# A hybrid encoder layer on one core: an operand split ahead, a transpose later, a gating step more, values loaded under the head before

## The chip, the cores and the metric

The kernel runs on one core of one Trainium2 chip. The metric is the time of one execution on the device in microseconds (us). The core has five engines with an instruction stream each, worked off in the order written: TensorE (PE in the profile; its weight loads are PEld), VectorE (DVE), ScalarE (ACT), GpSimd (POOL) and SyncE (SP). DMAs are issued from the streams of ACT, POOL and SP. An engine that meets an instruction whose semaphore has not come stands, and everything behind it in its stream stands too.

## The reference, cut to what matters

One layer over 1024 tokens (16 rows of 64 columns) with 2048 channels, float32:

```python
h = rms_norm(x, pre_g)
q, k, v, z_a, u, vs, z_b, g_a, g_b = split(h @ w_in)      # 1024 x 7 and 2048 x 2 columns
y_a = neighbourhood_attention(q, k, v, rpb) * silu(z_a)   # 8 heads of 128, window 8 x 16
y_b = u * (W_s layer_norm(vs) + b) * silu(z_b)            # 8 groups of 128, chunks of 128 tokens
merged = sigmoid(g_a) * (y_a @ w_pa) + sigmoid(g_b) * (y_b @ w_pb)
out = x + rms_norm(merged @ w_out, post_g)
```

## The kernel before, in words

Every float32 operand of the large products is split into a rounded part `wh` and a rest `wl` (ACT casts in line 120, DVE subtracts in line 121), and each product is made of three matmuls: high by high, high by low, low by high. A *step* is one such product of 512 contraction rows by 512 tokens: 12 matmuls in line 153. The columns of `w_in` are worked in pairs of 128; a pair takes 7 steps (a Strassen form with results in the PSUM banks A, B and C), a few pairs take 8 plain ones. There are 732 steps. After them the output projection runs in line 1001. The weights of a pair are loaded by SP a pair ahead (line 141), split two steps before their use, and results leave the banks by ACT (line 202, 292) and DVE (line 197); POOL's DMAs (line 293) store them to DRAM, the second half of the contraction being added there to the first.

The main loop (line 1024) writes one step after the other. In each it writes the evacuation of the step before, then for the first steps a piece of `first_builds` (the activations' operand tiles `a`: ACT scales `y` into the high part in line 411, DVE makes the low part in line 412), then one `hook()`, which advances the first of the waiting *tasks* up to its next `yield`, then the matmuls of the step, and then the split of weights two steps on. So a `yield` in a task is a distance of one step between what stands before and after it, on all engines at once. The tasks in order:

- `norms` (line 453): squares and sums of x, then `r_cols` = 1/rms by a DVE reduction (line 469) and a GpSimd power (line 116), then three small TensorE transposes (lines 473 and 483), DVE copies (475, 484), and a round trip over DRAM that spreads the result as `r_rows`.
- `values`, `layer_norms`: transposes of v and vs.
- `gating(g)` for 8 groups (line 557): loads `z` (a group ahead) and `u` from `d_zu`; first step: a matmul with `ones` (567) and z times r_rows (571); second step: Silu of z, the loads of the next group's z, and u times r_rows (578); third and fourth step: one half each of the chunk matmuls (583), the products (585, 587, 590) and the store. u is loaded by POOL (line 492) in the first step.
- `attention` (line 617): 8 heads, 11 steps each (`i` from 0 to 10): scores of block i (683), normalised (696), transposed (704) and, three steps after the scores, weighted with the values (716). A head's values come by four POOL loads (659) into one tile `vk`, issued ahead of `i` = 0. At `i` = 2 POOL loads the gate `za` (665), which DVE scales at `i` = 4 (751); at `i` = 3 it loads the next head's q and k, and from `i` = 7 on these are scaled and split (`prelude`).

```python
            fetch_values(h)
            following = None
            for i in range(11):
                if i >= 3:
                    weighted(h, i - 3)
```

`prepare_upto(k)` (line 1014) splits weights up to step k-1; before, the first call stands behind the first piece of `first_builds`.

Of the kernel before, what the change touches and what calls it, by code (L numbers as in the profile page):

```python
# [17 lines left out]
P = 128  # L18
# [75 lines left out]
def hybrid_kernel(ctx: ExitStack, tc: tile.TileContext, x, x_t, pre_g, post_g, w_vs, w_v, w_units, bias, ln_g, ln_b,  # L94
# [358 lines left out]
    def norms():  # L453
        pool = Pool(tc, "npool")
        ss = pool.tile([P, T // P, 2], F32, "ss")
        halves = {}
        for j in range(17):
            if j < 16:
                t, e = divmod(j, 2)
                halves[j] = pool.tile([P, T], F32, "xn", bufs=2)  # L460
                nc.sync.dma_start(out=halves[j], in_=x[t * P:(t + 1) * P, e * T:(e + 1) * T])
            yield
            if j > 0:
                t, e = divmod(j - 1, 2)
                src = halves.pop(j - 1)
                junk = pool.tile([P, T], BF16, "junk")
                nc.scalar.activation(junk, src, AF.Square, accum_out=ss[:, t, e:e + 1])
            yield
        nc.vector.tensor_reduce(out=r_cols, in_=ss, op=ALU.add, axis=AX.X)
        rsqrt_into(r_cols, r_cols, 1.0 / D, RMS_EPS)  # L470
        yield
        pt = psum("t")
        nc.tensor.transpose(out=pt[:T // P, :P], in_=r_cols, identity=ident)
        rows = pool.tile([T // P, P], F32, "rows")
        nc.vector.tensor_copy(rows, pt[:T // P, :P])
        nc.sync.dma_start(out=r_dram, in_=rows)
        nc.sync.dma_start(out=r_rows, in_=r_dram.rearrange("t p -> (t p)").partition_broadcast(P))

        for dst, src in ((lng, ln_g), (lnb, ln_b)):
            by_group = pool.tile([G, P], F32, "by_group", bufs=2)  # L480
            nc.scalar.dma_start(out=by_group, in_=src.rearrange("(g p) -> g p", p=P))
            pt = psum("t")
            nc.tensor.transpose(out=pt[:, :G], in_=by_group, identity=ident[:G, :G])
            nc.vector.tensor_copy(dst, pt[:, :G])
        yield
        pool.close()
# [62 lines left out]
    def fetch_group(g):  # L549
        z = [block(bpool, ("zu", g), 0, hf, "z", 4) for hf in range(2)]  # L550
        wst = bpool.tile([P, P], F32, "wst", bufs=2)
        nc.sync.dma_start(out=wst, in_=ws_t[:, g, :])
        bs = bpool.tile([P, 1, P], F32, "bs", bufs=2)
        nc.sync.dma_start(out=bs, in_=b_s[g:g + 1, :].partition_broadcast(P))
        fetched[g] = z, wst, bs

    def gating(g):

        if g not in fetched:
            fetch_group(g)  # L560
            yield
            yield
        z, wst, bs = fetched.pop(g)
        u = [block(bpool, ("zu", g), 1, hf, "u", 2) for hf in range(2)]

        pb = psum("t")
        nc.tensor.matmul(pb[:, :P], lhsT=ones, rhs=wst, start=True, stop=True)
        nc.vector.scalar_tensor_tensor(out=bs[:, 0], in0=pb[:, :P], scalar=lnb[:, g:g + 1], in1=bs[:, 0],
                                       op0=ALU.mult, op1=ALU.add)
        for hf in range(2):  # L570
            nc.vector.tensor_tensor(out=z[hf], in0=z[hf], in1=r_rows[:, hf * HALF:(hf + 1) * HALF], op=ALU.mult)
        yield
        for hf in range(2):
            nc.scalar.activation(z[hf], z[hf], AF.Silu)
        if ("zu", g + 1) in complete:
            fetch_group(g + 1)
        for hf in range(2):
            nc.vector.tensor_tensor(out=u[hf], in0=u[hf], in1=r_rows[:, hf * HALF:(hf + 1) * HALF], op=ALU.mult)
        yield
        for hf in range(2):  # L580
            po = psum("t")
            for i in range(4):
                nc.tensor.matmul(po[:, i * P:(i + 1) * P], lhsT=vn[hf * 4 + i][:, g * P:(g + 1) * P],
                                 rhs=wst, start=True, stop=True)
            nc.vector.tensor_tensor(out=u[hf], in0=u[hf], in1=z[hf], op=ALU.mult)
            yb = bpool.tile([P, HALF], F32, "yb", bufs=2)
            nc.vector.scalar_tensor_tensor(
                out=yb.rearrange("p (c s) -> p c s", s=P), in0=po.rearrange("p (c s) -> p c s", s=P),
                scalar=lng[:, g:g + 1], in1=bs.broadcast_to([P, 4, P]), op0=ALU.mult, op1=ALU.add)
            nc.vector.tensor_tensor(out=yb, in0=yb, in1=u[hf], op=ALU.mult)  # L590
            nc.gpsimd.dma_start(out=y_dram[8 + g][:, hf * HALF:(hf + 1) * HALF], in_=yb)
            yield
# [24 lines left out]
    def attention():  # L617

        pool = Pool(tc, "p2")
        scale = 128.0 ** -0.5  # L620
        raw, kept, bts = {}, {}, {}
        probs, sums, pv = {}, {}, {}

        def fetch(h):
# [27 lines left out]

            return [lambda: scaled(h, 0), lambda: queries(h), lambda: scaled(h, 1), lambda: keys(h)]

        def fetch_values(h):
            vk = pool.tile([P, 4, 4, P], F32, "vk")
            for b in range(4):
                w = KW[b]
                nc.gpsimd.dma_start(out=vk[:4 * w, b], in_=v_dram[h, :, COL0[b]:COL0[b] + w])
            kept[h].append(vk)  # L660

        def fetch_gate(h):
            zs = pool.tile([P, T], F32, "za")
# [44 lines left out]
        def weighted(h, i):  # L708
            hf, b = QTILES[i]
            n = 4 * KW[b]  # L710
            vk, zs = kept[h][2:]
            pk = probs.pop(("t", i))
            if b == 0:
                pv[hf] = psum("v")
            for rc in range(3):
                nc.tensor.matmul(pv[hf][:, b * P:(b + 1) * P], lhsT=vk[:n, b, ROW0[hf] // 4 + rc, :],  # L716
                                 rhs=pk[:n, rc, :], start=(rc == 0), stop=(rc == 2))
            if b == 3:
                zv = zs.rearrange("p (r b c) -> p b r c", b=4, c=16)[:, :, 8 * hf:8 * hf + 8]
                nc.vector.tensor_tensor(out=zv, in0=pv[hf].rearrange("p (b r c) -> p b r c", b=4, c=16),  # L720
                                        in1=zv, op=ALU.mult)

        for h in range(H):
            if h not in kept:
                while ("head", h) not in complete:
                    yield
                fetch(h)
                for i in range(3):
                    fetch_bias(h, i)
                    yield  # L730
                for f in prelude(h):
                    f()
                    yield
            fetch_values(h)
            following = None
            for i in range(11):
                if i >= 3:
                    weighted(h, i - 3)
                if 2 <= i < 10:
                    transposed(i - 2)  # L740
                if 1 <= i < 9:
                    normalised(i - 1)
                if i < 8:
                    if i < 5:
                        fetch_bias(h, i + 3)
                    scores(h, i)
                if i == 2:
                    fetch_gate(h)
                    zs = kept[h][3]
                if i == 4:  # L750
                    nc.vector.tensor_tensor(out=zs, in0=zs, in1=r_rows, op=ALU.mult)
                if i == 5:
                    nc.scalar.activation(zs, zs, AF.Silu)
                if i == 3 and ("head", h + 1) in complete:
                    fetch(h + 1)
                    following = prelude(h + 1)
                if following and i >= 7:
                    following[i - 7]()
                    if i >= 8:
                        fetch_bias(h + 1, i - 8)  # L760
                yield
            nc.gpsimd.dma_start(out=y_dram[h], in_=zs)
            del kept[h]
# [260 lines left out]
    for k, (n, name) in enumerate(seq):  # L1024
        for f, args in events.pop(k, ()):
            f(*args)
        if k:
            pn, pname = seq[k - 1]
            pairs[pn].evacuate(pname)
            release(k)  # L1030
        if not begun and next(starting, StopIteration) is StopIteration:
            begun = True
            ypool.close()
            begin(norms)
        if k % 4:
            build()
        need(pairs[n].left, PRODUCTS[name][1] if name in PRODUCTS else PlainPair.STEPS[name][1])
        hook()
        prepare_upto(k + 1)
        pairs[n].multiply(name)  # L1040
        prepare_upto(k + 1 + DEPTH)
        if k == len(seq) - 6:
            loaded.extend(load_chunk(n) for n in range(LOADS))
        if k == len(seq) - 1:
            advance(0)
# [163 lines left out]
```

## Time and profile before

| | |
|---|---|
| median of 3 runs | 2528.94 us (2527.4 to 2533.26) |
| the profiled execution | 2526.07 us |
| its span, first to last instruction | 2524.2 us |
| TensorE busy in it | 2485.5 us, 98% |
| VectorE / ScalarE / GpSimd busy | 56% / 42% / 17% |
| mean granted clock of TensorE | 0.996 |

The table is read so: TensorE is busy for nearly all of the span, so time is to be had only from the stretches in which it waits or has a lower clock. Its busy time does not tell the clock: a matmul at the lower level is busy for longer. The profiled execution took 1.9 us more than its span.

### The profile page before, as it was taken

Reading aid. Unit: us, or ns where it says so; the run is one execution under the profiler, and the core shown is the slowest. Engines: PE = TensorE matmul, PEld = TensorE weight load, DVE = VectorE, ACT = ScalarE, POOL = GpSimd, SP = SyncE. Lnnn points to the kernel's source line nnn. Section 1 sums busy time; section 2 is a strip of 40 time slices with the busy share of each in tenths; the row PEclk is TensorE's granted clock in tenths of the full one; section 3 lists DMA queues with packets and bytes.
Section 4 is the critical chain, followed back from the end, with each engine's and each line's share of the span. In section 5 each row is a group of like instructions: output and inputs, shape, how many; then the busy total and the mean of one; then the engine's idle time right before and its main releaser. Section 6 shows DMA issues by size and latency. Waiting matters only on the chain.

```text
span 2524.2 us, 32543 instructions
## 1 busy us (share of the span) xinstructions
PE 2485.5 (98%) x11363; PEld 2063.2 (82%) x11363; DVE 1421.7 (56%) x2284; ACT 1051.1 (42%) x1871; POOL 439.0 (17%) x669
## 2 busy tenths in 40 slices
PE   8999999999999999999999999999999999999998
PEld 6878888888888888887788878888888888888887
DVE  7444444444444754567765655566586787632434
ACT  5533333333334534443366656554443444432332
POOL 0111111111111112123322232233311121200000
PEclk9999999999999999999999999999999999999999
DMA  6643333333335469777778686799865687733635
GB/s 194 205 128 113 115 106 109 115 110 108 114 109 175 110 114 226 161 150 193 174 169 195 152 196 148 180 284 231 226 186 171 225 201 151 230 107 97 210 116 196
DMA packets 237380, 410.14 MB, mean 162 GB/s; under 512 B 31496, under 2 KB 90912, under 8 KB 236576
## 3 DMA queue, kind: packets, MB, share of 16 engines
q1 hardware_dynamic: 163296, 226.56, 30.3%
q0 software_dynamic: 72112, 176.77, 29.0%
q10 hardware_dynamic: 1808, 4.74, 0.5%
q8 instruction: 89, 1.46, 0.2%
q14 instruction: 75, 0.61, 0.1%
HBM read 264.78 MB, written 143.13 MB: 162 GB/s over the span
## 4 chain that ended last, share of the span: by engine, by line
PE 86%; issue 4%; DMA 4%; DVE 3%; ACT 2%; POOL 1%; POOLq 0%; SPq 0%; DVEq 0%; ACTq 0%
PE A L153 39%; PE C L153 20%; PE B L153 10%; PE t L1001 3%; PE A L1001 3%; PE v L1001 2%; PE s L1001 2%; PE C L1001 2%; PE B L1001 2%; DMA vk<-v_dram 1%; PE v L716 1%; DMA u<-d_zu 1%; DVE wl L121 1%; PE s L683 1%; PE t L516 1%
## 5 line engine op out<-in xcount | busy, mean ns | idle before, releaser
L153 PE MATMUL A<-a,wh 128*128 128x512 f32 x3328 | 1034.9, 392 | 10.4 <-ACT wh L120 9.2
L121 DVE TENSOR_TENSOR wl<-x,wh 128x512 fp32r<-128x512 f32 x736 | 505.8, 688 | 660.2 <-ACT wh L120 659.8
L153 PEld LDWEIGHTS A<-a,wh 128*128 128x128 f32 x3328 | 622.7, 189 | 136.1 <-ACT wh L120 9.2
L120 ACT CAST wh<-x 128x512 fp32r<-128x512 f32 x736 | 455.9, 620 | 488.2 <-PE C L153 229.0
L153 PE MATMUL A<-a,wl 128*128 128x512 f32 x1664 | 651.3, 391 | 1.7 <-DVE wl L121 1.7
L153 PE MATMUL C<-a,wh 128*128 128x512 f32 x1664 | 516.4, 392 | 3.5 <-DVE u L197 3.4
L202 ACT COPY u<-A 128x512 f32<-128x512 f32 x300 | 175.8, 586 | 537.3 <-PE A L153 534.9
L153 PEld LDWEIGHTS A<-a,wl 128*128 128x128 f32 x1664 | 313.6, 188 | 71.3 <-DVE wl L121 5.2
L153 PEld LDWEIGHTS C<-a,wh 128*128 128x128 f32 x1664 | 311.1, 188 | 67.0 <-issue 2.8
L153 PE MATMUL C<-a,wl 128*128 128x512 f32 x832 | 325.4, 391 | 2.8 <-DVE wl L121 2.7
L197 DVE TENSOR_TENSOR u<-C,u 128x512 f32<-128x512 f32 x200 | 137.9, 690 | 240.0 <-ACT u L202 149.1
L153 PE MATMUL B<-a,wh 128*128 128x512 f32 x864 | 267.2, 390 | 0.0
L153 PEld LDWEIGHTS B<-a,wh 128*128 128x128 f32 x864 | 161.2, 188 | 32.5
L153 PEld LDWEIGHTS C<-a,wl 128*128 128x128 f32 x832 | 156.6, 188 | 37.2 <-DVE wl L121 4.1
L153 PE MATMUL B<-a,wl 128*128 128x512 f32 x432 | 168.7, 390 | 0.2 <-DVE wl L121 0.2
L174 DVE TENSOR_TENSOR x<-x,x 128x512 f32<-128x512 f32 x200 | 137.7, 688 | 3.5
L120 ACT CAST wh<-s 128x512 fp32r<-128x512 f32 x100 | 62.1, 621 | 107.7 <-PE B L153 105.9
L292 ACT COPY c<-A 128x512 f32<-128x512 f32 x88 | 51.6, 586 | 127.0 <-PE A L153 127.0
L153 PEld LDWEIGHTS B<-a,wl 128*128 128x128 f32 x432 | 81.1, 188 | 18.3 <-DVE wl L121 1.2
L197 DVE TENSOR_TENSOR u<-B,u 128x512 f32<-128x512 f32 x100 | 68.8, 688 | 22.1 <-PE B L153 22.1
L1001 PE MATMUL A<-wh,a 128*128 128x512 f32 x208 | 80.9, 389 | 0.0
L1001 PE MATMUL t<-wh,a 128*128 128x512 f32 x208 | 80.9, 389 | 0.0
(241 smaller groups left out, 2546.0 us busy)
## 6 DMA issues: line engine op xcount, KB each, us to landing
x<-w_units SPq DMA_DIRECT2D x288, 256.0 KB, 2.9
x<-w_out SPq DMA_DIRECT2D x120, 256.0 KB, 2.7
d_zu<-u POOLq DMA_DIRECT2D x48, 256.0 KB, 4.0
d_qk<-u POOLq DMA_DIRECT2D x48, 256.0 KB, 4.0
d_gb<-u POOLq DMA_DIRECT2D x48, 256.0 KB, 3.6
d_ga<-u POOLq DMA_DIRECT2D x48, 256.0 KB, 4.1
m<-u POOLq DMA_DIRECT2D x48, 256.0 KB, 4.3
y<-x_t SPq DMA_DIRECT2D x32, 256.0 KB, 5.3
```

Source lines behind the costliest of these rows:

```text
L120: nc.scalar.copy(out=hi, in_=src)
L121: nc.vector.tensor_tensor(out=lo, in0=src, in1=hi.bitcast(F32), op=ALU.subtract)
L153: nc.tensor.matmul(acc, lhsT=wt[:, j * P:(j + 1) * P], rhs=operand[j // 2][:, j % 2, part], start=(first and j == 0 and n == 0), stop=(j = ...
L174: nc.vector.tensor_tensor(out=out, in0=in0, in1=in1, op=op)
L197: nc.vector.tensor_tensor(out=out, in0=in0, in1=out, op=ALU.add)
L202: nc.scalar.copy(out=u, in_=acc["A"])
L292: nc.scalar.copy(out=t, in_=bank)
L516: nc.tensor.transpose(out=pt[:, n * P:(n + 1) * P], in_=raws[i][:, n], identity=ident)
L683: nc.tensor.matmul(sv, lhsT=qs[:, a, hf, b], rhs=ks[:, c, rows, cols], start=(j == 0), stop=(j == 2))
L716: nc.tensor.matmul(pv[hf][:, b * P:(b + 1) * P], lhsT=vk[:n, b, ROW0[hf] // 4 + rc, :], rhs=pk[:n, rc, :], start=(rc == 0), stop=(rc == 2))
L1001: nc.tensor.matmul(acc[i], lhsT=stat[:, part, t * P:(t + 1) * P], rhs=wt, start=(kt == 0 and part == 0 and wt is chunk[0]), stop=(kt == nk ...
```

## The change

Four edits, none of which adds or removes arithmetic.

```diff
@@ norms @@
         rsqrt_into(r_cols, r_cols, 1.0 / D, RMS_EPS)
-        yield
+        for _ in range(4):
+            yield
         pt = psum("t")
@@ gating @@
         if ("zu", g + 1) in complete:
             fetch_group(g + 1)
+        yield
         for hf in range(2):
             nc.vector.tensor_tensor(out=u[hf], in0=u[hf], in1=r_rows[:, hf * HALF:(hf + 1) * HALF], op=ALU.mult)
@@ attention @@
-        def fetch_values(h):
-            vk = pool.tile([P, 4, 4, P], F32, "vk")
-            for b in range(4):
-                w = KW[b]
-                nc.gpsimd.dma_start(out=vk[:4 * w, b], in_=v_dram[h, :, COL0[b]:COL0[b] + w])
-            kept[h].append(vk)
+        def fetch_values(h, b):
+            if b == 0:
+                values_of[h] = []
+            vk = pool.tile([P, 4, P], F32, f"vk{b}")
+            w = KW[b]
+            nc.gpsimd.dma_start(out=vk[:4 * w], in_=v_dram[h, :, COL0[b]:COL0[b] + w])
+            values_of[h].append(vk)
...
-            fetch_values(h)
+                for b in range(4):
+                    fetch_values(h, b)
...
                 if following and i >= 7:
                     following[i - 7]()
+                    fetch_values(h + 1, i - 7)
@@ main loop @@
             release(k)
+        if k == 0:
+            prepare_upto(1)
         if not begun and next(starting, StopIteration) is StopIteration:
```

The four value loads of head 0 still stand together ahead of its `i` = 0; those of heads 1 to 7 stand at `i` = 7 to 10 of the head before, each into a tile of its own whose last reader (block b of the second half of the tokens) stands in the same step.

At the start, on ScalarE: `x_327` and `x_329` are the first two weight blocks, `a_0` and `a_1` the operand tiles from `y11`, the next two those from `y12`. Before:

```order
L141 DMA x_327<-w_v 128x4x128
L141 DMA x_329<-w_v 128x4x128
L411 ACTIVATE a_0_415<-y_0_317,g_cols 128x512 x2
L411 ACTIVATE a_1_420<-y_1_322,g_cols 128x512 x2
L120 CAST wh<-x_327 128x512
L120 CAST wh<-x_329 128x512
L411 ACTIVATE a_0_450<-y_0_318,g_cols 128x512 x2
```

and now:

```order
L141 DMA x_327<-w_v 128x4x128
L141 DMA x_329<-w_v 128x4x128
L120 CAST wh<-x_327 128x512
L411 ACTIVATE a_0_423<-y_0_317,g_cols 128x512 x2
L411 ACTIVATE a_1_428<-y_1_322,g_cols 128x512 x2
L120 CAST wh<-x_329 128x512
L411 ACTIVATE a_0_450<-y_0_318,g_cols 128x512 x2
```

The cast of the first weights now stands ahead of the four operand pieces of the first product. VectorE's stream changes in the same way: the first `wl` stands ahead of the first low parts.

In the gating, on VectorE, from the first instructions of a group to its first half (`wl`, `x` and the banks' `u` are the steps' own work). Before:

```order
L568 SCALAR_TENSOR_TENSOR bs<-t,lnb,bs 128x128
L571 TENSOR_TENSOR z<-z,r_rows 128x512 x2
L121 TENSOR_TENSOR wl<-s_9215,wh 128x512
L197 TENSOR_TENSOR u_9192<-C,u_9192 128x512
L578 TENSOR_TENSOR u<-u,r_rows 128x512 x2
L121 TENSOR_TENSOR wl<-x_9053,wh 128x512
L585 TENSOR_TENSOR u<-u,z 128x512
```

and now:

```order
L569 SCALAR_TENSOR_TENSOR bs<-t,lnb,bs 128x128
L572 TENSOR_TENSOR z<-z,r_rows 128x512 x2
L121 TENSOR_TENSOR wl<-x_9053,wh 128x512
L121 TENSOR_TENSOR wl<-x_9207,wh 128x512
L174 TENSOR_TENSOR s_9418<-x_9209,x_9270 128x512
L174 TENSOR_TENSOR x_9209<-x_9207,x_9209 128x512
L580 TENSOR_TENSOR u<-u,r_rows 128x512 x2
L121 TENSOR_TENSOR wl<-x_9097,wh 128x512
L197 TENSOR_TENSOR u_9439<-C,u_9439 128x512
L587 TENSOR_TENSOR u<-u,z 128x512
```

The work of one more step stands between z times r_rows and u times r_rows.

In the attention, on GpSimd, from the end of the second head to the gate loads of the third. Before:

```order
L293 DMA d_qk_2_162<-c_11275 128x512
L293 DMA d_qk_0_164<-u_11236 128x512
L293 DMA d_qk_1_161<-u_11095 128x512
L762 DMA y_dram_69<-za 128x1024
L659 DMA vk<-v_dram 96x1x512
L659 DMA vk<-v_dram 128x1x512 x2
L659 DMA vk<-v_dram 96x1x512
L293 DMA d_qk_3_167<-u_11458 128x512
L665 DMA za<-d_za_0_184 128x512
L665 DMA za<-d_za_1_185 128x512
```

and now:

```order
L293 DMA d_qk_2_162<-c_11281 128x512
L662 DMA vk_11307<-v_dram 96x1x512
L293 DMA d_qk_0_164<-u_11242 128x512
L662 DMA vk_11347<-v_dram 128x1x512
L293 DMA d_qk_1_161<-u_11101 128x512
L662 DMA vk_11380<-v_dram 128x1x512
L662 DMA vk_11411<-v_dram 96x1x512
L767 DMA y_dram_69<-za 128x1024
L293 DMA d_qk_3_167<-u_11467 128x512
L668 DMA za<-d_za_0_184 128x512
L668 DMA za<-d_za_1_185 128x512
```

The value loads stand among the stores of the head before and ahead of its result `y_dram`; between that result and the gate loads one store is left.

## Rows read from the trace of the kernel before

**Rows 1.** The page's first part: busy us (share of span) xinstructions, for TensorE.

```profile
PE 2485.5 (98%) x11363; PEld 2063.2 (82%) x11363; DVE 1421.7 (56%) x2284; ACT 1051.1 (42%) x1871; POOL 439.0 (17%) x669
```

**Rows 2.** TensorE's waits: who waited for whom, us in total, times, longest us.

```profile
PE A L153 <- ACT wh L120: 9.2, 1, 9.2
PE v L716 <- DMA vk<-v_dram: 6.3, 3, 2.7
PE C L153 <- DVE u L197: 3.4, 2, 1.9
PE C L153 <- DVE wl L121: 2.7, 2, 2.0
...
PE t L473 <- POOL r_cols L116: 1.7, 1, 1.7
```

**Rows 3.** Stretches: length, TensorE busy (instructions), granted clock, DMA share, GB/s.

```profile
150.05:153.46 3.41, 3.41 (x10) 0.50 0.03 6
...
1508.55:1511.97 3.42, 3.42 (x10) 0.50 1.04 290
```

**Rows 4.** The chain of waits: start, us, piece; two steps of 12 matmuls.

```profile
141.45 2.73 PE A L153 x12
149.50 4.54 PE A L153 x12
```

**Rows 5.** Timeline of the start: start, us, engine, instruction, count [idle <-releaser].

```profile
1.25 0.96 ACTq L141 DMA_DIRECT2D x<-w_v  x2
...
7.93 0.72 ACT L411 ACTIVATE a<-y,g_cols 128x512 fp32r<-128x512 f32 x1 [0.77 <-DMA y<-x_t]
8.56 1.12 ACT L120 CAST wh<-x 128x512 fp32r<-128x512 f32 x2
8.69 0.75 DVE L412 SCALAR_TENSOR_TENSOR a<-y,g_cols,a 128x512 fp32r<-128x512 f32 x1 [0.74 <-ACT a L411]
...
10.69 1.05 PE L153 MATMUL A<-a,wh 128*128 128x512 f32 x2
...
25.19 0.59 ACT L292 COPY u<-A 128x512 f32<-128x512 f32 x1 [4.48 <-PE A L153]
```

**Rows 6.** Timeline round the transposes of `norms`.

```profile
146.37 2.21 POOL L116 TENSOR_TENSOR r_cols<-r_cols,neghalf 128x8 f32<-128x8 f32 x1
...
156.67 0.62 ACT L120 CAST wh<-s 128x512 fp32r<-128x512 f32 x1 [1.49 <-PE B L153]
156.84 0.69 DVE L197 TENSOR_TENSOR u<-B,u 128x512 f32<-128x512 f32 x1 [0.33 <-PE B L153]
```

**Rows 7.** Stretches of the gating, as in group 3: one group, then the five behind it.

```profile
1129.13:1142.07 12.94, 12.94 (x69) 1.00 0.88 235
1142.07:1218.88 76.81, 69.91 (x331) 0.98 0.70 180
```

**Rows 8.** Timeline of one group's u: its loads and its multiplication.

```profile
1147.34 1.44 POOL L492 DMA_DIRECT2D u<-d_zu  x2
...
1153.48 1.44 DVE L578 TENSOR_TENSOR u<-u,r_rows 128x512 f32<-128x512 f32 x2 [4.34 <-DMA u<-d_zu]
```

**Rows 9.** Stretches of the attention: head 1, then heads 2 to 7.

```profile
1276.07:1318.06 41.99, 41.99 (x231) 1.00 0.73 168
1318.06:1585.38 267.32, 257.45 (x1371) 0.99 0.73 174
```

**Rows 10.** DMA issues, 1400 to 1600 us: count, KB each, median us to landing.

```profile
vk<-v_dram POOLq DMA_DIRECT2D x10, 256.0 KB, 10.2
za<-d_za POOLq DMA_DIRECT2D x10, 256.0 KB, 9.2
```

**Rows 11.** VectorE's waits for u and for the gate, and SyncE's longest in the attention.

```profile
DVE u L578 <- DMA u<-d_zu: 23.6, 9, 4.3
...
DVE za L751 <- DMA za<-d_za: 6.1, 3, 3.5
...
SPq L141 <- DVE wl L121: 129.4, 23, 12.7
```

More of the change, by code (lines that the diff above doesn't have):

```diff
@@ L620, in attention @@
         scale = 128.0 ** -0.5
-        raw, kept, bts = {}, {}, {}
+        raw, kept, bts, values_of = {}, {}, {}, {}
         probs, sums, pv = {}, {}, {}
@@ L710, in weighted @@
             n = 4 * KW[b]
-            vk, zs = kept[h][2:]
+            zs, vk = kept[h][2], values_of[h][b]
             pk = probs.pop(("t", i))
@@ L715, in weighted @@
             for rc in range(3):
-                nc.tensor.matmul(pv[hf][:, b * P:(b + 1) * P], lhsT=vk[:n, b, ROW0[hf] // 4 + rc, :],
+                nc.tensor.matmul(pv[hf][:, b * P:(b + 1) * P], lhsT=vk[:n, ROW0[hf] // 4 + rc, :],
                                  rhs=pk[:n, rc, :], start=(rc == 0), stop=(rc == 2))
@@ L748, in attention @@
                     fetch_gate(h)
-                    zs = kept[h][3]
+                    zs = kept[h][2]
                 if i == 4:
```

## The prediction

> **What bounds the kernel now.** I read the page's busy times first: TensorE is busy for 98% of the span [rows 1], so no edit away from it gains anything unless TensorE waits there. Then its waits: the reader is to see that each long one falls into a stretch that one of the four edits touches: 9.2 us for the first weights, 6.3 us for the values, 3.4 and 2.7 us for VectorE in the C products, 1.7 us for `r_cols` [rows 2]. The waits are not all that is lost. The granted clock falls to 0.50, the lower of its two levels, for 3.41 us in four places from 150 to 1512 us, each right behind such a wait [rows 3]; a step takes 4.54 us there instead of 2.73 [rows 4]. Half a stretch, 1.7 us, is lost each time. So I went on by stages and compared stretches of equal work, since their lengths hold waits, clock and small gaps together. Two ends hold nothing for this change: the projection and the evacuations there.
>
> **The start.** TensorE's first matmul waits 9.2 us [rows 2], because the first cast stands behind the four operand pieces, the last of which starts at 7.93, when its data has come [rows 5]. The first weights were asked for at 1.25 us, and other blocks of 256 KB asked for a little later are used by 7.93 [rows 5]; I take 5.5 us for their landing, the middle between 3 and 8. Then the cast ends at about 6.1 and the first operand piece (0.7 us each) at 6.8, where TensorE starts, 2.4 us earlier than at 9.2. It cannot run away: the last operand piece still starts at about 8 and its low part ends near 9.4 [rows 5], so the first product ends at 10.5 at the earliest instead of 14. Its first matmuls go at 425 ns (two in the 0.85 us from 10.69) against 227 ns later (2.73 by 12, [rows 4]), so a start earlier by 2.4 us is worth only 1.2 if the faster pace still comes at the same moment, and up to 3.3 if it comes earlier too. I take 2.4. It is kept afterwards: ScalarE, idle for 4.48 us before the first evacuation, waits for TensorE there [rows 5], and VectorE's builds hang on that evacuation, so all of it moves forward together.
>
> **The norms.** The power on POOL takes 2.21 us from 146.37 [rows 6]; TensorE stands 1.7 us for it and then pays 1.8 us of clock (4.54 less 2.73, [rows 4]), with 0.2 us of pipeline restart: 3.7. Three steps more, 8.2 us, cover the power. What is late next: the transposes now stand right behind a C product whose addition VectorE does first, for 0.69 us as the B addition of 156.84 [rows 6]. The copy of the first transposed block stands behind it, and the third transpose needs that copy's buffer, so TensorE waits some 0.7 us there. The two small loads by ScalarE could be late too; they now stand behind the cast that starts at 156.67, released by the B product [rows 6], one product (2.7 us) ahead of TensorE's need; I cost them at nothing, and at 1.5 us if that cover fails. Gain 3.7 - 0.7 = 3.0; with the clock's stretch coming back 1.3. The later `r_rows` is first used in the gating, hundreds of us on.
>
> **The gating.** A group without disturbance takes 12.94 us, the five behind it 76.81 [rows 7]: 76.81 - 5 x 12.94 = 12.1 us lost, one stretch of low clock among them. The cause is in VectorE's stream: u is asked for at 1147.34 and multiplied at 1153.48 after 4.34 us of idling [rows 8]; nine such waits come to 23.6 us [rows 11], and weight splits and bank additions queue behind each. The added step puts 2.7 us or more between, so of the longest wait 1.6 is left. VectorE also gets more room: the eight groups take 40 steps for 32, and a group's eleven gating instructions on VectorE (0.7 us or less each, by the 1.44 for two, [rows 8]) lie beside 15.7 us of steps (12.94 and 2.73) and not 12.9. What is late next is the remaining wait for u, which the splits' lead of two steps covers. I take 11.1 gained and leave 1.0; the bounds are 5 (the wait comes back in the two or three longest groups) and 12.1. The eight steps cost nothing at the far end: the attention's first scores stand in the same step as before, since it waits for head 0's columns.
>
> **The attention.** Head 1 takes 41.99 us, the six behind it 267.32 [rows 9]: 267.32 - 6 x 41.99 = 15.4 us lost. 6.3 us are waits for values [rows 2], two low clock stretches [rows 3] add 3.4, and most of the rest follows the gate: VectorE waits 6.1 us for `za` [rows 11], whose load stands in POOL's queue behind the four value loads and lands after 9.2 us [rows 10]. The values land after 10.2 us [rows 10], used from the fourth step on, 3 x 3.8 = 11.4 us behind their issue (41.99 by 11 steps): no room. Asked for at steps 7 to 10 of the head before, each has at least seven steps, some 27 us. The gate loads then follow the stores alone. The moved load waits for the weighted product of its own step; behind it on POOL stand only stores whose results come later, so I cost that at nothing. The Trainium skill, "DMA: Bandwidth & Descriptors", section on the anatomy of one DMA (SWDGE), gives about 2.0 us and bytes by 436 GB/s, 2.6 us for a block of 256 KB. By that rule the values would be there before their use, the edit would remove nothing, and the sum below would be 14.4 us smaller; the trace disagrees, 10.2 us, and the sum goes by the trace. I take 14.4 of the 15.4, leaving 1.0 for ScalarE's table loads round the gate's Silu; bounds 6 and 15.4.
>
> **The sum.** 2.4 + 3.0 + 11.1 + 14.4 = 30.9 us. The profiled execution took 2526.07 us (span 2524.2 and 1.9 around it), 2.9 us less than the median of the three runs, 2528.94; so 2495.2 by the profile's own time and 2498.0 by the median. I say 2497.
>
> **The rivals.**
> - *The wait for u stays* (late loads queue behind POOL's stores, which follow VectorE): for it, POOL's u loads come only after a store that waits; against it, the waits are all shorter than a step and a half. The gating gives 5 and not 11: 2503.
> - *The attention keeps its stalls in another place* (the gate still late, or ScalarE behind): for it, the gate's load also has to follow the store of the head before; against it, head 1, whose values also come four at once, has no loss. It gives 6 and not 14.4: 2505.
> - *The stalls move rather than go*: each edit leaves a wait and with it a stretch of low clock; half of everything comes back, 15 us: 2512.
> - *Slower*: the moved value loads land on the queue and the DMA engines at the end of a head, where the next head's biases, q, k and the weights are due; TensorE then waits for weights once a load. It decides from (30.9 - 14.4) by 28 loads, 0.6 us a load, on; at 1.2 us the 28 loads cost 34, and without the 14.4 the time is 2529 + 34 - 16.5 = 2546. Against it: SyncE waits up to 12.7 us for a free weight buffer [rows 11], so weights are asked for as soon as there is room and well ahead, and no engine waits for them in the attention now.
> - *No change*: the edits only shift idle time because something else ends last. Against it, there is no other engine above 56% [rows 1].
>
> **How the numbers follow.** Forecast (2490 to 2502) 0.70; the wait for u stays 0.10; the attention keeps its stalls 0.08; stalls move 0.06; slower 0.03; no change 0.03. The likeliest gives 2497. Its own bounds are 2488 (3.3 at the start, all of the other losses, with the profile's offset) and 2502; taking in the first two rivals and part of the third, the range is 2488 to 2509. A measurement of this kernel can tell 0.2%, 5 us, from no change: faster 0.94, same 0.03, slower 0.03.
>
> **What would show it.** Right: TensorE's first wait near 7 us; no waits for `vk` and `r_cols`; heads 2 to 7 at 42 to 43 us each; VectorE's waits for u under 2 us each, and five steps of gating at 15.6 us; no stretch at 0.50 between 20 us and the end but for one or two. A wait of about 0.7 us before the third small transpose. Wrong: waits of TensorE for weights or for POOL at the ends of heads, u still waited for by 3 us, or low clock stretches at new places.

## The result and the profile after

The changed kernel takes 2496.99 us (median of 4 runs, 2495.95 to 2497.88), the kernel before, run beside it, 2528.17 us (4 runs, 2524.31 to 2533.26). The ratio is 0.9878 with a 95% interval of 0.9865 to 0.9891: faster by 31.2 us. The forecast was 2497. The profiled execution took 2496.82 us with a span of 2495.04, 29.14 less than the span of before.

Where they went is read from the steps of twelve matmuls into which the program falls. The first matmul of each step is found in both traces, and lengths between the same steps are compared. (The first matmul of step 0 is TensorE's first of all; a gating or attention stretch begins and ends with a step too.)

| stage | before | after | gain | forecast |
|---|---|---|---|---|
| start, to step 40 | 122.25 | 120.61 | 1.64 | 2.4 |
| norms, steps 40 to 54 | 42.55 | 39.52 | 3.03 | 3.0 |
| steps 54 to 398, not touched | 951.40 | 951.41 | -0.01 | 0 |
| gating, steps 398 to 446 | 159.87 | 149.61 | 10.26 | 11.1 |
| attention, steps 446 to 534 | 350.85 | 336.87 | 13.98 | 14.4 |
| the rest | 897.27 | 897.02 | 0.25 | 0 |

The gains add up to 29.15, the difference of the spans. The 344 steps in the middle, which nothing touches and in which TensorE does not wait, agree within 0.01 us, so the cutting itself adds nothing. A stage with waits in it varies by more from one execution to the next, as the experiments show.

The page's first part after (busy us, share of the span, instructions) answers to [rows 1]:

```profile
PE 2474.6 (99%) x11363; PEld 2060.1 (83%) x11363; DVE 1422.5 (57%) x2284; ACT 1051.4 (42%) x1871; POOL 439.9 (18%) x669
```

The instructions are as many as before. TensorE is busy for 10.9 us less, although it does the same matmuls. A matmul at the lower clock counts as busy for longer, and the four stretches at 0.50, 13.65 us together, are gone: that is 6.8 us. The other 4.1 were not traced to a cause. The remaining 18 us are time in which TensorE stood.

TensorE's waits after (who waited for whom, us in total, times, longest), for [rows 2]:

```profile
PE A L153 <- ACT a L411: 7.0, 1, 7.0
PE C L153 <- DVE u L197: 1.5, 1, 1.5
PE t L484 <- DVE rows L476: 0.7, 1, 0.7
PE A L153 <- ACT u L202: 0.7, 1, 0.7
PE A L153 <- DVE wl L121: 0.7, 1, 0.7
...
```

The first wait is now for the first operand piece and not for the weights; `vk` and `r_cols` are gone from the list; of the waits for u's addition one of 1.5 us is left.

Stretches of TensorE after (from, to, length, busy and instructions, granted clock, share of the DMA engines, GB/s): the norms, the whole gating, one undisturbed group of it and the one disturbed, head 1, and heads 2 to 7. They answer to [rows 3, 7, 9]:

```profile
120.61:160.13 39.52, 38.81 (x172) 1.00 0.51 158
1111.54:1261.15 149.61, 147.96 (x725) 1.00 0.79 197
1127.19:1142.85 15.66, 15.66 (x82) 1.00 0.77 204
1158.50:1176.50 18.00, 16.35 (x81) 1.00 0.71 164
1261.15:1303.23 42.08, 42.08 (x230) 1.00 0.76 179
1303.23:1556.48 253.25, 252.69 (x1370) 1.00 0.74 184
```

The granted clock is 1.00 in all of them; the four stretches at 0.50 of [rows 3] have gone with the waits ahead of them. Heads are counted from 1 here and in the prediction, so head 1 is the code's head 0. Heads 2 to 7 take 42.2 us each, about as long as head 1, which had lost nothing before.

### The profile page after: what moved, and what is told of

Its sections match the earlier page's. It is cut to its first block, busy times and chain, and to the rows that moved or that the text cites. A ratio compares the mean times of both kernels' runs of the same rounds, so it can differ in the third digit from the quotient of the medians.

```text
span 2495.0 us, 32575 instructions
## 1 busy us (share of the span) xinstructions
PE 2474.6 (99%) x11363; PEld 2060.1 (83%) x11363; DVE 1422.5 (57%) x2284; ACT 1051.4 (42%) x1871; POOL 439.9 (18%) x669
## 4 chain that ended last, share of the span: by engine, by line
PE 88%; issue 6%; POOL 2%; DVE 1%; DMA 1%; ACT 1%; POOLq 0%; DVEq 0%; ACTq 0%
PE A L153 40%; PE C L153 20%; PE B L153 10%; PE t L1006 3%; PE A L1006 3%; PE v L1006 2%; PE s L1006 2%; PE C L1006 2%; PE B L1006 2%; PE v L719 2%; PE s L686 1%; POOL g_gb L802 1%; PE t L707 1%; DMA u<-d_zu 1%; POOL d_ga L293 1%
```

## The experiments

Twelve kernels ran in three sets of four, each set beside runs of the kernel before (medians 2526.0, 2527.3 and 2527.51 us). They ask three things: whether the four parts add up and each is worth what its stage shows; what makes the gating faster, the longer lead of u's loads or the room that a fifth step gives VectorE; and whether the values or the gate `za` cost the attention its time.

**One part alone.** Four kernels are the kernel before with one hunk of the change each.

```diff
# only_start
+        if k == 0:
+            prepare_upto(1)
# only_norms
-        yield
+        for _ in range(4):
+            yield
# only_gating
             fetch_group(g + 1)
+        yield
         for hf in range(2):
# only_values: vk in four tiles, loaded at steps 7 to 10 of the head before
```

> The kernel before with the first edit alone (first weights split ahead of the operand). Theory: the four edits act each in its own stage and add up; then this one gives what the first stage of the changed kernel gave, 1.6 us (first matmul 2.2 us earlier, first product 0.5 us longer), and the other stages keep the lengths of before to within 0.5 us each. Rival: the start's gain is taken back at the waits for VectorE near 42 and 46 us, or the changed kernel's start was earlier by chance of when the faster clock came: 0 to 0.5 us.

> The kernel before with the second edit alone (transposes of the norms four steps on). Theory: 3.0 us less in the steps from 40 to 54, of which 1.7 to 1.8 are the stretch at granted clock 0.50 that follows the wait; a wait of 0.7 us for the copy of the rows remains. Rival: the stretch at 0.50 comes behind any wait there and moves with it: 1.3 us less.

> The kernel before with the third edit alone (gating in five steps). Theory: 10.3 us less from the first gating step to the first scores (steps 398 to 446), and the attention as before, head 1 at 42 us and heads 2 to 7 at 267 us together. Rival: part of the attention's gain came from the gating (a different moment of its start against the DMA queues): the attention changes by 2 us or more.

> The kernel before with the fourth edit alone (values in four tiles under the head before). Theory: 14 us less in heads 2 to 7, the waits of TensorE for values gone, VectorE's waits for the gate under 1 us in total, gating as before. Rival: the gate's waits were the gating's or the clock's doing, not the value loads': about 10 us less and VectorE still waits 6 us for the gate.

| kernel | median us | ratio [95%] | start | norms | gating | attention |
|---|---|---|---|---|---|---|
| before, its profile | | | 122.25 | 42.55 | 159.87 | 350.85 |
| only_start | 2525.21 | 0.9998 [0.9988, 1.0008] | 119.87 | 42.52 | 159.87 | 355.68 |
| only_norms | 2525.52 | 0.9997 [0.9985, 1.0008] | 122.28 | 39.50 | 162.85 | 350.64 |
| only_gating | 2514.76 | 0.9954 [0.9938, 0.9970] | 121.77 | 42.53 | 148.33 | 347.84 |
| only_values | 2515.85 | 0.9963 [0.9950, 0.9976] | 121.89 | 42.53 | 163.03 | 337.79 |

By the whole time two of them are a miss: neither the start nor the norms can be told from no change, and the four medians add up to 22.7 us, not to 31.2. By the stages each does about what it does in the full change, 2.38, 3.05, 11.54 and 13.06 us, 30.0 in all. What differs stands in the table: a stage that a kernel leaves alone doesn't keep its length. The untouched gating takes 159.87 to 163.03 us, the untouched attention 347.84 to 355.68, since TensorE's waits there hang on when a DMA lands. The runs of before beside these four spread from 2518.78 to 2531.46, and two or three us are lost in that. So the parts add up by stages of single traces; that they add up by the whole time is not shown.

Two expectations missed in their details. The attention of only_gating is 3.0 us shorter than before, past the 2 us that its rival named; but where nothing touched it, it took from 349.32 (u_ahead_four_steps, below) to 355.68 us, so this decides nothing. In only_values heads 2 to 7 lose the 14.0 us that were expected, but VectorE still waits 1.7 us for the gate, and the gating, 3.2 us longer, takes part of it back.

The rows of only_start show it. TensorE's waits, the first matmul's between two of the attention:

```profile
PE v L716 <- DMA vk<-v_dram: 8.0, 4, 3.7
PE A L153 <- ACT a L411: 6.9, 1, 6.9
...
PE v L716 <- DVE sm L695: 3.8, 3, 1.7
```

Its first matmul starts about as early as after the full change, at 6.9 us, and its attention waits 8.0 us for values where the profile of before has 6.3 [rows 2].

**What makes the gating faster.** Three kernels part lead from room. In step_behind_u, on the kernel before, the fifth step stands behind u's multiplication, not ahead of it: as much room, no lead. In u_ahead_four_steps, also on before, each half of the next group's u is asked for right behind the store of the half that frees its buffer: lead, no room. u_ahead_five_steps is the changed kernel with that edit as well.

```diff
# step_behind_u
             nc.vector.tensor_tensor(out=u[hf], in0=u[hf], in1=r_rows[:, ...], op=ALU.mult)
         yield
+        yield
# u_ahead_four_steps, u_ahead_five_steps
-    fetched = {}
+    fetched, ahead = {}, {}
-        u = [block(bpool, ("zu", g), 1, hf, "u", 2) for hf in range(2)]
+        u = ahead.pop(g, None) or [block(bpool, ("zu", g), 1, hf, "u", 2) for hf in range(2)]
             nc.gpsimd.dma_start(out=y_dram[8 + g][:, hf * HALF:(hf + 1) * HALF], in_=yb)
+            if g + 1 in fetched:
+                ahead.setdefault(g + 1, []).append(block(bpool, ("zu", g + 1), 1, hf, "u", 2))
```

> The kernel before with a fifth gating step that stands behind the multiplication of u and not ahead of it, so that u is loaded one step ahead as before but VectorE gets the same room of five steps a group. Theory A (the room does it): about 10 us less from step 398 to 446, as in the changed kernel, though VectorE waits for u as in the kernel before, some 24 us. Theory B (the wait for u does it): under 4 us less. Between them, both count.

> The kernel before with four gating steps, but the next group's u is loaded in the last two steps of the group before, each half behind the half that frees its tile. So u has one to two steps more, as in the changed kernel, without more room. Theory A (room): under 4 us less from step 398 to 446, VectorE's waits for u under 10 us. Theory B (wait): about 10 us less.

> The changed kernel with u loaded ahead as well. The changed kernel still has VectorE waiting 15.2 us for u and one wait of TensorE of 1.5 us there. Theory A and B alike: VectorE's waits for u under 3 us, TensorE's wait gone, 1.5 to 2 us less than the changed kernel. Rival: the loads, behind the stores of yb on POOL, come no earlier: as the changed kernel.

| kernel | median us | ratio [95%] | gating | VectorE's waits for u: sum, times, longest |
|---|---|---|---|---|
| before | | | 159.87 | 23.6, 9, 4.3 |
| step_behind_u | 2520.31 | 0.9977 [0.9966, 0.9988] | 154.23 | 21.4, 8, 4.7 |
| u_ahead_four_steps | 2517.12 | 0.9960 [0.9946, 0.9975] | 150.97 | 15.2, 7, 2.9 |
| the changed kernel | 2496.99 | 0.9878 [0.9865, 0.9891] | 149.61 | 15.2, 9, 3.2 |
| u_ahead_five_steps | 2494.31 | 0.9872 [0.9855, 0.9888] | 147.23 | 1.1, 1, 1.1 |

Room alone gives 5.6 us of gating, and the same step put ahead of u's multiplication 10.3 to 11.5 (after, only_gating), so its place is worth another 5 or 6 beside its being there: between the two theories, both count. The early request alone gives 8.9, and with the step 12.6; it leaves VectorE 15.2 us of waits where under 10 were expected. That room does it all is refuted by step_behind_u, as far as one trace of each goes: its gating is 5.9 us longer than only_gating's, more than the 3.2 by which the untouched gating differs between executions, while the intervals of the two whole times just overlap. That lead does it all is not refuted as firmly: u_ahead_four_steps is 1.4 to 2.6 us behind the kernels with the step in its gating, less than those 3.2, and by the whole time its interval and only_gating's overlap.

In step_behind_u one group still makes TensorE wait, with a stretch at the lower clock in it. TensorE's wait, then that group and the whole gating, as in the stretches above:

```profile
PE C L153 <- DVE u L197: 3.5, 1, 3.5
```

```profile
1148.02:1168.98 20.96, 17.48 (x81) 0.92 0.65 168
...
1116.43:1270.66 154.23, 150.20 (x724) 0.99 0.79 191
```

In u_ahead_five_steps VectorE waits for u once, for 1.1 us, and TensorE never stands in the whole gating; its length is its busy time:

```profile
1110.99:1258.22 147.23, 147.23 (x725) 1.00 0.82 200
```

**Values or gate.** In gate_later, on the kernel before, the values stay as they are and the multiplication of `za` comes one step later.

```diff
-                if i == 4:
+                if i == 5:
                     nc.vector.tensor_tensor(out=zs, in0=zs, in1=r_rows, op=ALU.mult)
```

> The kernel before with the scaling of the gate at step 5 of a head and not 4; the loads are untouched. Theory: the losses of heads 4 and 7 (2.1 and 1.7 us) come from VectorE waiting for the gate, which the value loads hold up on their queue: heads 4 and 7 at 42 to 42.5 us, the waits for values (heads 2, 5 and 6) as before, some 3 to 4 us less in all. Rival: what holds up heads 4 and 7 is ScalarE with its table loads for the gate's Silu: no gain, or a loss, as the Silu now follows its scaling within a step.

It took 2523.45 us, 0.9989 [0.9980, 0.9999], and VectorE's wait for `za` is gone from the list. The waits for values remain:

```profile
PE v L716 <- DMA vk<-v_dram: 6.7, 3, 3.2
```

They stand in heads 2, 5 and 6, as before. Heads 4 and 7, in which VectorE had waited 3.49 and 2.43 us for `za` and TensorE not for values, took 44.12 and 43.72 us before; now they lose nothing more:

```profile
1406.92:1449.26 42.34, 42.24 (x231) 1.00 0.75 186
...
1541.73:1583.70 41.97, 41.97 (x231) 1.00 0.77 188
```

So in those two heads the late gate was the whole loss, 3.5 us of the 14. The rest hangs on the values: in only_values, where values and gate are both in time, heads 2 to 7 take what they take after the full change, 253.31 us against 253.25, and the one wait for the gate that is left is in head 1, whose values are asked for late as before:

```profile
1321.78:1575.09 253.31, 252.74 (x1371) 1.00 0.75 184
```

```profile
DVE za L753 <- DMA za<-d_za: 1.7, 1, 1.7
```

A kernel with four tiles that are all asked for at the head's start was not run; whether the splitting gives anything without the earlier request stays open.

**One part less, in the quiet kernel.** Since the kernel after spreads by about 2 us and not by ten, the small parts can be weighed there. without_start and without_norms are the change less that hunk; after_again is the changed kernel once more beside them, and both_further adds to u_ahead_five_steps that the norms' two small loads are asked for at the task's start and the transposes come one step later still.

```diff
# both_further, in norms
-        halves = {}
+        halves, small = {}, []
+        for dst, src in ((lng, ln_g), (lnb, ln_b)):
+            by_group = pool.tile([G, P], F32, "by_group", bufs=2)
+            nc.scalar.dma_start(out=by_group, in_=src.rearrange("(g p) -> g p", p=P))
+            small.append((dst, by_group))
...
-        for _ in range(4):
+        for _ in range(5):
             yield
```

> The changed kernel once more, as a measure for the three others on the same chip. Expected 2495 to 2498 us, runs within 3 us of each other, where the kernel before spreads over 10 us and more.

> The changed kernel less its first edit (first weights split behind the first operand pieces again). Alone, that edit could not be told from noise by the whole time, since the gating and attention of the kernel before vary by several us from run to run. Theory: those variations are gone here, and the 1.6 us of the start show: the median 1.2 to 2.2 us above the changed kernel's. Rival: the start's gain is given back later also here: within 0.5 us of the changed kernel.

> The changed kernel less its second edit (transposes of the norms right behind the power again). Theory: 2.5 to 3.5 us above the changed kernel, with a wait of 1.7 us for r_cols and a stretch at granted clock 0.50 behind it. Rival: the time is given back in gating and attention, as the profile of that edit alone seemed to show: within 1 us of the changed kernel.

> The changed kernel with u loaded ahead in the gating (the two halves in the last two steps of the group before) and the norms' transposes one step further on, where no bank addition stands ahead of the copy of the rows, their two small loads moved to the start of the task. Theory: 2.3 us less in the gating and 0.4 us less at the transposes (the wait of 0.7 us for the rows down to 0.2): 2494, 2 to 3.5 us below the changed kernel. Rival: moving the small loads or the transposes adds a wait elsewhere: no better than with u ahead alone, 2494.3 or above.

| kernel | median us (lowest, highest) | ratio [95%] | start | norms | gating |
|---|---|---|---|---|---|
| after_again | 2496.05 (2495.12, 2497.36) | 0.9879 [0.9865, 0.9894] | 120.03 | 39.52 | 149.59 |
| without_start | 2499.24 (2498.16, 2499.33) | 0.9892 [0.9875, 0.9909] | 122.09 | 39.52 | 148.92 |
| without_norms | 2499.29 (2498.41, 2500.20) | 0.9892 [0.9877, 0.9907] | 121.33 | 40.92 | 150.67 |
| both_further | 2493.64 (2492.96, 2494.32) | 0.9869 [0.9855, 0.9884] | 120.50 | 39.01 | 147.23 |

Each of the two parts is now worth 3.2 us by the medians, and no run of either kernel without it is as short as the longest of after_again. For the start that is more than was expected and more than its own stage shows, 2.06 (122.09 less 120.03); the spans of the two profiled runs differ by 2.17. The run of without_start that has a trace is the shortest of its four, 1.1 us below their median, so the rest lies in runs without one.

For the norms the profile is odd in another way. The wait for `r_cols` is back as it was, and yet the stage is only 1.40 longer than in after_again, not 3.0:

```profile
PE t L473 <- POOL r_cols L116: 1.7, 1, 1.7
```

```profile
121.33:162.25 40.92, 38.96 (x173) 1.00 0.48 155
```

That is 1.40 of the 4.20 us by which the two profiled spans differ. Another 1.30 lie in the start, which this kernel does not change and in which the faster pace came at 13.43 us, not at 11.0 as in after_again; 1.08 lie in the gating. So that the norms' part is worth 3.2 us rests on the whole times alone.

In this execution no stretch at 0.50 follows the wait. In the seven others with the same 1.7 us wait (the kernel before and six of the experiments) one does, and the stage is 42.5 long.

both_further is the shortest kernel of the study, 2.4 us ahead of after_again by the medians; ahead of u_ahead_five_steps, 0.7 us in another set, it can't be told by the whole time. Its norms are 0.5 shorter, and the third transpose's wait for `rows` is down to 0.2:

```profile
PE t L486 <- DVE rows L480: 0.2, 1, 0.2
```

## Why the prediction was right, point by point

**The start: right, the term 0.8 too large in the profile.** The weights' wait gave way to the operand piece, as forecast. The start of the program after (start, us, engine, instruction, idle before and its releaser), for [rows 5]:

```profile
5.74 0.62 ACT L120 CAST wh<-x 128x512 fp32r<-128x512 f32 x1 [3.05 <-DMA x<-w_v]
6.27 2.71 ACT L411 ACTIVATE a<-y,g_cols 128x512 fp32r<-128x512 f32 x4
...
7.04 1.58 PE L153 MATMUL A<-a,wh 128*128 128x512 f32 x2 [7.04 <-ACT a L411]
...
11.40 0.97 PE L153 MATMUL A<-a,wh 128*128 128x512 f32 x2
...
12.45 0.62 PE L153 MATMUL B<-a,wh 128*128 128x512 f32 x2
```

The weights were cast from 5.74 and the first matmul started at 7.04 (forecast 6.8). The first product took 5.41 us (7.04 to 12.45) where before it took 4.87 (9.21 to 14.08), so of 2.18 us 1.64 are left. The working had named this: the slow pace of 425 ns a matmul holds until a moment of its own, and the faster one came at 12.14 here, at 13.52 before, at 11.0 in after_again, whose start stage gained 2.22. The bounds of 1.2 and 3.3 hold all of these. Over the fourteen traces the start takes 121.77 to 122.49 us in the eight without the edit and 119.87 to 121.33 in the six with it. So the gain is shown, and its size in one execution depends on when the faster pace comes: in the shortest of the six it came at 10.77 us, in the longest at 13.43.

**The norms: right, 3.03 for 3.0, with the wait that was to come.** The transposes after, for [rows 6]:

```profile
153.25 0.27 PE L474 MATMUL t<-ident,r_cols 128*8 128x128 f32 x1
153.45 0.69 DVE L197 TENSOR_TENSOR u<-C,u 128x512 f32<-128x512 f32 x1 [1.43 <-PE C L153]
154.06 0.27 DVE L476 COPY rows<-t 8x128 f32<-8x128 f32 x1
154.38 0.22 PE L484 MATMUL t<-ident,by_group 8*128 8x8 f32 x1 [0.71 <-DVE rows L476]
```

The first transpose follows its C product without a wait; VectorE's addition of 0.69 us goes ahead of the copy, and the third transpose waits 0.71 for it: the 0.7 of the sum. (Before, it waited for `rows` by 0.2 us, as much as the working added for a restart.) No stretch at 0.50 followed this wait, here or in the four other traces that have it. The small loads, asked for at 150.58, held nothing up.

**The gating: the size right, a step of the working wrong.** The forecast said that the added step puts 2.7 us or more between u's request and its use, so that of the longest wait 1.6 would be left, and that waits of 3 us would prove it wrong. They were there. VectorE's waits after, for [rows 11]:

```profile
DVE u L580 <- DMA u<-d_zu: 15.2, 9, 3.2
DVE za L755 <- DMA za<-d_za: 0.8, 1, 0.8
```

Two things in the working were wrong: what the step adds to the lead, and that u lands as long after its request as before. The lead is the time from the start of the request on POOL to VectorE's arrival at the multiplication (the start of that less its idling). For groups 2 to 8 it was 1.2 to 3.8 us before, 2.4 in the mean, and is now 2.5 to 5.8, 4.3 in the mean: 1.9 more and not 2.7. In the group of [rows 8], the third, it grew from 1.8 to 4.7, by all that was forecast, but u landed 7.9 us behind its request and not 6.1, so that 3.15 us of waiting are left:

```profile
1144.56 1.47 POOL L493 DMA_DIRECT2D u<-d_zu  x2
...
1152.41 1.40 DVE L580 TENSOR_TENSOR u<-u,r_rows 128x512 f32<-128x512 f32 x2 [3.15 <-DMA u<-d_zu]
```

In step_behind_u and without_norms this group's load took 7.2 and 8.4 us too, in the kernels of four steps that left the loads alone 5.7 to 6.4; why it lands later is not shown. The fourth group is the one that is still disturbed. Its rows before, the request and the multiplication:

```profile
1163.38 1.40 POOL L492 DMA_DIRECT2D u<-d_zu  x2
...
1168.48 0.69 DVE L578 TENSOR_TENSOR u<-u,r_rows 128x512 f32<-128x512 f32 x1 [3.92 <-DMA u<-d_zu]
```

And after, the request, then VectorE's stream from z's multiplication on:

```profile
1162.40 1.44 POOL L493 DMA_DIRECT2D u<-d_zu  x2
...
1161.71 1.29 DVE L572 TENSOR_TENSOR z<-z,r_rows 128x512 f32<-128x512 f32 x2
1162.91 0.69 DVE L121 TENSOR_TENSOR wl<-x,wh 128x512 fp32r<-128x512 f32 x1
1163.51 0.69 DVE L174 TENSOR_TENSOR x<-s,x 128x512 f32<-128x512 f32 x1
1164.21 0.69 DVE L121 TENSOR_TENSOR wl<-x,wh 128x512 fp32r<-128x512 f32 x1
1168.07 0.69 DVE L580 TENSOR_TENSOR u<-u,r_rows 128x512 f32<-128x512 f32 x1 [3.18 <-DMA u<-d_zu]
1170.66 0.69 DVE L580 TENSOR_TENSOR u<-u,r_rows 128x512 f32<-128x512 f32 x1 [1.90 <-DMA u<-d_zu]
```

A step is 2.73 us to TensorE, but to VectorE, when it has nothing to wait for, it is what VectorE has to do in it. Before, one weight split stood between the two multiplications; now the difference of two weight blocks (line 174) and a second split stand there too, 1.3 us. The lead went from 1.2 us (1168.48 less 3.92 of idling, less 1163.38) to 2.5, and u landed 5.1 us behind the request before and 5.7 now. This group is the one that still cost TensorE 1.53 us:

```profile
1176.50 0.71 PE L153 MATMUL C<-a,wh 128*128 128x512 f32 x2 [1.53 <-DVE u L197]
```

That the gating gained 10.3 nevertheless is the second half of the term, which the forecast gave no price of its own: the eight groups have a quarter more steps for the same work of VectorE's, so a wait of 3 us leaves it still ahead of TensorE in all groups but this one, where two waits came to 5.1. Before, VectorE's waits of 2.85 and 2.87 us in the fifth and seventh group cost TensorE 1.5 and 1.9 us, the two waits for u's addition of [rows 2]; now those of 3.15 and 3.23 in the third and sixth cost it nothing. The runs show both halves (5.6 us for room alone, 8.9 for lead alone), which overlap. step_behind_u has the room without the lead: its mean lead is 2.4 us, as before. How long a wait VectorE can bear is no fixed number: in step_behind_u 4.18 and 0.71 in one group cost TensorE at most 0.5, 4.68 in the next cost 3.5. An undisturbed group of five steps took 15.66, as forecast (15.6).

**The attention: right, 13.98 for 14.4.** No wait for values, heads 2 to 7 at 42.2 each (forecast 42 to 43). The DMA issues of 1372 to 1572 us after (count, KB each, median us from issue to landing), for [rows 10]:

```profile
vk<-v_dram POOLq DMA_DIRECT2D x10, 256.0 KB, 8.6
...
za<-d_za POOLq DMA_DIRECT2D x10, 256.0 KB, 5.1
```

The values still take 8.6 us, spread over four steps (10.2 when four came at once); they are in time because they are asked for at least seven steps ahead, some 27 us. The gate's load, no longer behind them, lands after 5.1 and not 9.2, and VectorE waits 0.8 us for it in place of 6.1: the step "the gate loads then follow the stores alone". gate_later shows what the wait for the gate was worth by itself. Of the 15.4 us that heads 2 to 7 lost, 1.3 are left, in heads 5 and 6 (42.67 and 42.60); the forecast put 1.0 down to ScalarE's table loads, and no run tests that. The figure worked out from the Trainium skill, "DMA: Bandwidth & Descriptors", section on the anatomy of one DMA (SWDGE), an estimate of 2.6 us for a block of 256 KB, does not agree with the trace here either; by it the edit would have removed nothing, and it removed 14 us.

**The rivals.** The wait for u did stay in VectorE's rows, but in TensorE's, where it counts, only once: 10.3 gained, not 5. The stalls of the attention did not stay, and none moved: between 20 and 2490 us TensorE has no stretch at 0.50. The slower case needed TensorE to wait for weights at the ends of heads; its longest wait for a split in the whole program is 0.7 us. The 31.2 us of the medians against 29.1 of the profiles is the profiled run of before, 2526.07, which lies 2.1 below the median of before; the forecast lay between its two sums for this reason, 2495.2 and 2498.0.

**The sum: right, and to the hundredth by luck.** The terms are 1.8 us too large together by the profiles (30.9 for 29.15) and 0.3 too small by the medians, and the profile of before happens to have a short gating: where nothing touched it, the gating took 159.87 to 163.03 us, before 159.87. The bounds are not all worked out: 2488 comes out only if the profile's 2.9 us are taken off a second time (2526.07 less 34.5 is 2491.6), and the terms' lower bounds, 13.5 us together, would give some 2514 and not 2502. The measured time tests neither.

## What to carry to other kernels

Price a step put between a load and its use by what the waiting engine does in that step (1.9 us of lead in the mean here), not by the bound engine's time for it (2.73), and don't count on the load to land as soon after its request as before; what lead the step doesn't give has to come from asking earlier. Stages of equal work, cut at the same matmul in both traces, show parts of 2 us that the whole time hides behind its own spread; and it is in the kernel whose waits are gone that a part left out can be weighed. A transfer that an engine waits for may be late because of what stands ahead of it in its queue, so look at the neighbour (`za` behind `vk`) before moving its user.

## What the runs showed of the hardware that was not expected

The same wait of 1.7 us was followed by a stretch at the granted clock of 0.50 in seven profiles and not in the eighth. The stage took 3.0 us more than without the wait in the first (the kernel before) and 1.4 in the last. The wait's length alone doesn't tell it: in the kernel before, TensorE's waits of 1.53, 1.87 and 1.49 us at 1190, 1216 and 1461 us were not followed by one, nor was one of 3.0 us in only_norms, at 1216.

The spread of the times went with the waits for the values: side by side the kernel before ran from 2521.11 to 2530.21 us (7 runs), the changed kernel from 2495.12 to 2497.36 (4 runs). only_values, whose gating waits for u as before, ran within 2.1 us (5 runs), and only_gating, whose attention waits for values as before, within 8.0 (6 runs). The runs are few, and which landings vary was not traced.
